# Moving the compressed projections, splitting a gate, and preparing branch weights one tile ahead in a one-core decoder trunk

## The chip, the cores and the metric

The kernel runs on one core of one Trainium2 chip. The metric is the device time of one execution in microseconds (us). TensorE (PE) multiplies, VectorE (DVE), ScalarE (ACT) and GpSimd (POOL) do the elementwise work, and SyncE (SP) issues most of the transfers from and to device memory. Everything is float32; nearly every matrix product is made of three products of rounded halves (a high part `hi` and the remainder `lo`), so each weight matrix has to be split by two instructions before it can be used: a cast on ACT that makes `hi`, and a subtraction that makes `lo`.

## The reference

One layer over 1024 tokens of width 1024: RMS norm, one input projection, three attention branches, a gated merge, an output projection, then a gated convolutional feed-forward. What the change touches is this:

```
kc = compress_blocks(k_cmp): blocks of 32 tokens, stride 16, + position; gelu(flat @ w1) @ w2
vc = compress_blocks(v_cmp): the same with its own weights
g = sigmoid(gates)                       # 3 x 1024 channels
merged = g0 * (y_a @ w_pa) + g1 * (y_b @ w_pb) + g2 * (y_c @ w_pc)
x = x + merged @ w_o
```

`y_a`, `y_b` and `y_c` are 256, 384 and 384 wide.

## The kernel before

Features lie on the partitions and tokens along the free axis, in two halves of 512. The program has stages in this order: an opening (norm, transposes), the input projections in pairs, the compressed projections with their two MLPs, attention, the branch outputs (`branch`, L1751), the last two gates, the merge (`merge`, L1766), the output projection, the feed-forward.

Inside the attention stage, and in a few others, the order of each engine's instructions is written out by a planner in the kernel (`Flow`), and TensorE's order there is fixed by it. In the compressed stage, and from the branch outputs to the first half of the output projection, the framework orders each engine's instructions instead: it takes them by their place in the program, but lets a later one go first when it expects an earlier one not to be ready. All orders are fixed when the kernel is built; on the chip each engine and each queue runs its own list in order.

`dense` (L784) takes the next 128 columns of the input projection's weights, which `next_w` has split one step ahead, and makes two halves of 24 products of 512 columns each, into the two PSUM banks with the tag `dn`. `dense_fm` (L302), which the merge uses, takes its banks from a rotation over all eight instead (`bank_tile`, L291).

**The compressed stage** (L2208 to L2212) is: `compress_in(0)` (project k, then split it into eight operands), `compress(0)` (its MLP), `compress_in(1)` (project v), `gate(2)`, `compress(1)`. `compress` (L1502) loads the 2 MB of first-layer weights in four parts. A part goes into a tile `raw` (tag `q1`, two buffers), is cast into `k1` and its remainder put into `k2` (two buffers each), and then feeds 12 products of 256 columns. After the fourth part come GELU, two transposes, a copy, two small products and a few copies. The tags `q1`, `q2`, `k1`, `k2`, `v`, `pc` and `p0` to `p5` are those of the attention stage: its first loads of queries, keys and values wait until the compressed stage has given these buffers up. Attention's own TensorE list begins with gate 3 (`fill`, products at L1700) and then the first scores.

**The merge** runs over eight tiles of 128 output columns. For each tile and each branch, `wprep` (L266) loads the branch's weights (SP), casts them (ACT, L274) and subtracts (POOL, L276), with two buffers each for `wr`, `wh` and `wl`. The gate's 128 x 1024 values are loaded into `gr` (three buffers; SP, L1773) and go through a sigmoid (ACT, L1774). The branch's products follow, 12 or 18 of 512 columns, and for each half of the tokens one or two instructions on DVE (L1780, L1782, L1783). The third branch ends with a cast and a subtraction that write the merged operand (L1785, L1786). In tiles 2 to 5 `wo_part` (L1790) also loads, casts and subtracts (POOL, L1796) a quarter of the first half of `w_o`; the second half follows after the merge.

Of the kernel before, what the change touches and what calls it, by code (L numbers as in the profile page):

```python
# [6 lines left out]
F32 = mybir.dt.float32  # L7
F32R = mybir.dt.float32r
BF16 = mybir.dt.bfloat16
AF = mybir.ActivationFunctionType  # L10
ALU = mybir.AluOpType
# [4 lines left out]
P = 128  # L16
# [217 lines left out]
class Trunk:  # L234
# [548 lines left out]

    def dense(self, evac):  # L784
        w = self.next_w()
        for hh in range(2):
            ps = self.psA.tile([P, 512], F32, "dn")
            for k in range(8):
                self.mm3(ps, (w[0][:, k], w[1][:, k]), (self.hT[hh][0][:, k], self.hT[hh][1][:, k]), k == 0, k == 7)
            evac(hh, ps)  # L790
# [675 lines left out]
    def compress_in(self, which):  # L1466

        nc = self.nc
# [23 lines left out]
        for x in range(2):  # L1492
            for y in range(2):
                fv = fs[x].rearrange("p a g c -> p (a g c)")[:, y * 512:y * 512 + 512]
                f = self.ap.tile([P, 2, 512], F32R, f"p{2 * x + y}")
                fh, fl = f[:, 0], f[:, 1]
                nc.scalar.copy(fh, fv)
                nc.vector.tensor_tensor(fl, fv, fh.bitcast(F32), ALU.subtract)
                out.append((fh, fl))
        return out  # L1500

    def compress(self, which, fq):  # L1502

        nc, ap = self.nc, self.ap
# [5 lines left out]
        for p4 in range(4):  # L1510
            raw = ap.tile([P, 4, 256], F32, "q1")
            hi = ap.tile([P, 4, 256], F32R, "k1")
# [150 lines left out]

    def gate(self, f):

# [10 lines left out]

        self.dense(evac)

# [87 lines left out]
    def merge(self, pool, ys, f, out):  # L1766

        nc, a = self.nc, self.a
        acc = pool.tile([P, S], F32, "acc")
        for br, (w, kk) in enumerate(((a["w_pa"][0], 2), (a["w_pb"][0], 3), (a["w_pc"][0], 3))):  # L1770
            wt = self.wprep([w[:, f * P:(f + 1) * P]], kk, P)
            gt = pool.tile([P, S], F32, "gr")
# [14 lines left out]

            self.dense_fm(wt, lambda k, hh: (yh[:, k, hh * 512:hh * 512 + 512], yl[:, k, hh * 512:hh * 512 + 512]), kk, evac)

    def wo_part(self, wo, nh, k):  # L1790
# [4 lines left out]
        nc.scalar.copy(wo[0][:, k:k + 2], raw)  # L1795
        nc.gpsimd.tensor_tensor(wo[1][:, k:k + 2], raw, wo[0][:, k:k + 2].bitcast(F32), ALU.subtract)  # L1796

# [388 lines left out]
    def run(self):  # L2186
# [20 lines left out]
        self.wspec = wl  # L2207
        fq = self.compress_in(0)  # L2208
        self.compress(0, fq)
        fq = self.compress_in(1)  # L2210
        self.gate(2)
        self.compress(1, fq)  # L2212
        self.psum_pool(True)
# [119 lines left out]
```

## Time and profile before

| | us |
|---|---|
| median of 3 runs (lowest, highest) | 1694.63 (1693.8, 1695.72) |
| the profiled execution | 1694.78 |
| its span (first to last instruction) | 1693.0 |
| busy: TensorE, VectorE, ScalarE, GpSimd | 1644.5, 1306.0, 835.7, 419.1 |

The profile lists instructions with start and duration, and gives the idle time ahead of one on its engine with what ended it. A product's end is modelled; the spacing of starts tells more. Products of 512 columns that follow one another at full clock start 0.23 us apart while each is shown 0.39 us long, so a gap of 0.6 us between two starts is a loss of some 0.4 us, of which the trace calls only 0.2 idle.

### The profile page before, as it was taken

To read this page: it belongs to the slowest core of one execution; us is meant where nothing else is said; L and a number is where in the kernel's file an instruction comes from. 1 tells how busy PE (TensorE), PEld (TensorE's weight loads), DVE (VectorE), ACT (ScalarE), POOL (GpSimd) and SP (SyncE) were. 2 spreads that over 40 slices of the span, in tenths; PEclk is the share of its full clock that TensorE was granted. 3 is DMA by queue.
4 is the path that set the end of the run, shared out by engine and by line. 5 is a ranking of instruction groups with operands and counts; after the bars stand their busy time and mean duration, and the time that the engine had idled before them with its cause. 6 is when DMAs were issued, how large, how long until landed. Compare 5 with 4: busy or idle time off the path is not lost.

```text
span 1693.0 us, 24484 instructions
## 1 busy us (share of the span) xinstructions
PE 1644.5 (97%) x8456; PEld 1367.5 (81%) x8456; DVE 1306.0 (77%) x2292; ACT 835.7 (49%) x1612; POOL 419.1 (25%) x323
## 2 busy tenths in 40 slices
PE   6989999998999999999999999999999999999998
PEld 6878888877888888888876788888888888888886
DVE  8976676553888889889477427999999999865774
ACT  6433443223878877788544314433333333454461
POOL 2232322321000011110034300165555645100020
PEclk9999999999999999999999999999999999999999
DMA  6545665367467664671466600255445544487671
GB/s 206 157 121 153 171 172 164 106 157 187 111 163 186 161 165 116 167 206 52 143 218 207 246 28 13 75 184 171 169 146 186 183 157 147 159 262 229 207 256 51
DMA packets 226058, 269.10 MB, mean 159 GB/s; under 512 B 21184, under 2 KB 162070, under 8 KB 225726
## 3 DMA queue, kind: packets, MB, share of 16 engines
q1 hardware_dynamic: 223262, 259.52, 51.5%
q0 software_dynamic: 1088, 4.88, 0.9%
q10 hardware_dynamic: 1584, 3.15, 0.5%
q8 instruction: 67, 1.10, 0.3%
q14 instruction: 57, 0.47, 0.1%
HBM read 188.26 MB, written 81.93 MB: 160 GB/s over the span
## 4 chain that ended last, share of the span: by engine, by line
PE 62%; DVE 21%; issue 6%; DMA 5%; ACT 3%; POOL 1%; SPq 0%; DVEq 0%; POOLq 0%; ACTq 0%
PE X L1700 6%; PE dn L298 5%; PE dn L299 5%; PE dn L300 5%; PE S L300 4%; PE S L299 4%; PE S L298 4%; PE X L1150 4%; DVE t L1975 3%; PE T L300 3%; PE T L298 3%; PE T L299 3%; DVE u L2036 2%; PE PV L1197 2%; PE S L1052 2%
## 5 line engine op out<-in xcount | busy, mean ns | idle before, releaser
L1169 DVE TENSOR_TENSOR tl<-X,th 128x512 fp32r<-128x512 f32 (+2 forms) x202 | 116.5, 586 | 14.9 <-ACT th L1166 12.7
L1166 ACT CAST th<-X 128x512 fp32r<-128x512 f32 (+2 forms) x202 | 101.3, 508 | 34.8 <-PE X L1150 31.9
L1736 POOL TENSOR_TENSOR wl<-wr,wh 128x256 fp32r<-128x256 f32 x44 | 33.5, 794 | 307.4 <-ACT wh L1731 292.6
L1076 DVE TENSOR_REDUCE sm<-S 128x1 f32<-128x640 f32 (+7 forms) x128 | 87.6, 712 | 22.0 <-PE S L1052 21.1
L1975 DVE SCALAR_TENSOR_TENSOR t<-u,ccols,t 128x511 f32<-128x511 f32 (+1 forms) x88 | 94.4, 1072 | 6.6 <-ACT t L1970 5.5
L1150 PE MATMUL X<-ident,p 128*128 128x128 f32 x610 | 97.7, 275 | 0.5 <-DVE tl L1169 0.3
L1084 ACT ACTIVATE p<-S,sm 128x640 f32<-128x640 f32 (+7 forms) x128 | 90.7, 713 | 13.6 <-DVE sm L1076 12.9
L1196 PE MATMUL PV<-th,v 128*128 128x256 f32 (+1 forms) x362 | 94.3, 283 | 0.1
L1052 PE MATMUL S<-k,q 98*128 98x128 f32 (+6 forms) x240 | 89.6, 382 | 1.0 <-issue 1.0
L1197 PE MATMUL PV<-tl,v 128*128 128x256 f32 (+1 forms) x362 | 89.5, 281 | 0.6 <-DVE tl L1169 0.5
L1048 PE MATMUL S<-k,q 128*128 128x512 f32 (+2 forms) x240 | 81.5, 340 | 2.2 <-ACT p L1084 2.1
L1150 PEld LDWEIGHTS X<-ident,p 128*128 128x128 f32 x610 | 70.3, 140 | 8.3 <-DVE tl L1169 1.0
L1700 PE MATMUL X<-hTh,wh 128*128 128x512 f32 x176 | 73.7, 419 | 2.2 <-DVE vcs L1551 2.1
L1900 POOL TENSOR_TENSOR su<-wr 128x512 f32<-128x512 f32 x20 | 32.1, 1606 | 168.6 <-DMA wr<-w_up 76.4
L276 POOL TENSOR_TENSOR wl<-wr,wh 128x384 fp32r<-128x384 f32 (+2 forms) x29 | 39.6, 1369 | 136.0 <-ACT wh L274 113.3
L1700 PE MATMUL X<-hTh,wl 128*128 128x512 f32 x176 | 73.1, 415 | 0.0
L1700 PE MATMUL X<-hTl,wh 128*128 128x512 f32 x176 | 72.9, 414 | 0.0
L1197 PEld LDWEIGHTS PV<-tl,v 128*128 128x128 f32 x362 | 68.5, 189 | 4.9 <-DVE tl L1169 1.9
L1196 PEld LDWEIGHTS PV<-th,v 128*128 128x128 f32 x362 | 68.5, 189 | 4.0 <-DVE y L1217 2.2
L1976 ACT ACTIVATE t<-t 128x512 f32<-128x512 f32 x44 | 27.8, 633 | 83.9 <-DVE t L1975 83.9
L298 PE MATMUL dn<-hTh,wh 128*128 128x512 f32 x152 | 59.7, 393 | 2.8 <-ACT f L1672 2.1
L300 PE MATMUL S<-blk,wh 128*128 128x512 f32 x152 | 60.1, 395 | 0.2 <-DVE wh L1912 0.2
(817 smaller groups left out, 5533.6 us busy)
## 6 DMA issues: line engine op xcount, KB each, us to landing
wr<-w_up SPq DMA_DIRECT2D x66, 256.0 KB
gr<-dg SPq DMA_DIRECT2D x24, 512.0 KB
t<-w_down SPq DMA_DIRECT2D x22, 512.0 KB
dt<-t SPq DMA_DIRECT2D x22, 512.0 KB
wr<-w_in SPq DMA_DIRECT2D x40, 256.0 KB
wr<-dl SPq DMA_DIRECT2D x39, 256.0 KB
wr<-w_in SPq DMA_DIRECT2D x18, 512.0 KB
x<-x SPq DMA_DIRECT2D x16, 512.0 KB
```

Source lines behind the costliest of these rows:

```text
L298: nc.tensor.matmul(out, st[0], mv[0], start=first, stop=False)
L299: nc.tensor.matmul(out, st[0], mv[1], start=False, stop=False)
L300: nc.tensor.matmul(out, st[1], mv[0], start=False, stop=last)
L1052: nc.tensor.matmul(out, q.t[1][0:R, qs], k.t[1][0:R, cs], start=False, stop=True)
L1084: nc.scalar.activation(o.rearrange("p a b -> p (a b)"), u, AF.Exp, bias=mx[:, x:x + 1], accum_out=sm[:, 2 + x:3 + x])
L1150: nc.tensor.transpose(ps[:, n * P:(n + 1) * P], b(), self.ident)
L1166: nc.scalar.copy(g.th[:, cs], ps[:, cs])
L1169: yield "DVE", 0, 0.07 + cs.stop * 1.04e-3, lambda: nc.vector.tensor_tensor(g.tl[:, cs], ps[:, cs], g.th[:, cs].bitcast(F32), ALU.subtract)
L1196: nc.tensor.matmul(unit.pv[:, oc], w, g.th[:, cs], start=first and i == 0, stop=False)
L1197: nc.tensor.matmul(unit.pv[:, oc], w, g.tl[:, cs], start=False, stop=e)
L1700: nc.tensor.matmul(p, w[i][:, k], self.hT[hh][j][:, k], start=x == 0, stop=x == 23)
L1975: nc.vector.scalar_tensor_tensor(o, i, cw[2 - sh], o, ALU.mult, ALU.add)
```

## The change

`compress_in` runs for k and for v before either MLP; the operands of v get buffers of their own (tags `q2` and `v`). The second half of gate 2 comes after the MLP of v in the program, the first half ahead of it. The MLP's raw weights take four buffers (`q1` and `pc`, two each) in place of two. `dense` takes its banks from the rotation. In the merge, the three branches' weights of a tile are one operand, loaded by three transfers, cast by one instruction and subtracted by one on DVE; it is made after the first branch's products of the tile before. `wo_part` subtracts on DVE.

```diff
-    def dense(self, evac):
+    def dense(self, evac, between=None):
         w = self.next_w()
         for hh in range(2):
-            ps = self.psA.tile([P, 512], F32, "dn")
+            if hh and between:
+                between()
+            ps = self.bank_tile()
...
-                f = self.ap.tile([P, 2, 512], F32R, f"p{2 * x + y}")
+                f = self.ap.tile([P, 2, 512], F32R, (f"p{2 * x + y}", ("q2", "v")[x])[which])
...
-            raw = ap.tile([P, 4, 256], F32, "q1")
+            raw = ap.tile([P, 4, 256], F32, ("q1", "pc")[p4 // 2])
...
-        for br, (w, kk) in enumerate(((a["w_pa"][0], 2), (a["w_pb"][0], 3), (a["w_pc"][0], 3))):
-            wt = self.wprep([w[:, f * P:(f + 1) * P]], kk, P)
+        if f == 0:
+            self.merge_weights(0)
+        hi, lo = self.mw
+        for br, (k0, kk) in enumerate(((0, 2), (2, 3), (5, 3))):
+            wt = hi[:, k0:k0 + kk], lo[:, k0:k0 + kk]
...
+            if br == 0 and f < 7:
+                self.merge_weights(f + 1)
+
+    def merge_weights(self, f):
...
+        raw = self.wp.tile([P, 8, P], F32, "wr")
+        for n, k0, k1 in (("w_pa", 0, 2), ("w_pb", 2, 5), ("w_pc", 5, 8)):
+            nc.sync.dma_start(raw[:, k0:k1], a[n][0][:, f * P:(f + 1) * P].rearrange("(k p) n -> p k n", p=P))
+        self.mw = hi, lo = self.wp.tile([P, 8, P], F32R, "wh"), self.wp.tile([P, 8, P], F32R, "wl")
+        nc.scalar.copy(hi, raw)
+        nc.vector.tensor_tensor(lo, raw, hi.bitcast(F32), ALU.subtract)
...
-        nc.gpsimd.tensor_tensor(wo[1][:, k:k + 2], raw, wo[0][:, k:k + 2].bitcast(F32), ALU.subtract)
+        nc.vector.tensor_tensor(wo[1][:, k:k + 2], raw, wo[0][:, k:k + 2].bitcast(F32), ALU.subtract)
...
-        fq = self.compress_in(0)
-        self.compress(0, fq)
-        fq = self.compress_in(1)
-        self.gate(2)
-        self.compress(1, fq)
+
+        fq = [self.compress_in(x) for x in range(2)]
+        self.compress(0, fq[0])
+        self.gate(2, lambda: self.compress(1, fq[1]))
```

## Rows read from the trace of the kernel before

**Rows 1.** The page's first part: busy time, share of the span and instructions of each engine.

```profile
PE 1644.5 (97%) x8456; PEld 1367.5 (81%) x8456; DVE 1306.0 (77%) x2292; ACT 835.7 (49%) x1612; POOL 419.1 (25%) x323
```

**Rows 2.** Windows of 20 us: length, busy time and instructions of PE, PEld, DVE, ACT, POOL, then TensorE's granted clock (1.00 is 2.4 GHz), busy share of the transfer engines, GB/s.

```profile
360.00:380.00 20.00, 18.53 (x97) 15.32 (x97) 15.05 (x31) 7.33 (x9) 2.67 (x3) 1.00 0.84 192
400.00:420.00 20.00, 15.85 (x73) 12.97 (x74) 3.96 (x7) 2.73 (x7) 2.52 (x2) 0.91 0.89 209
...
840.00:860.00 20.00, 16.25 (x70) 12.46 (x69) 11.10 (x12) 11.45 (x15) 3.23 (x4) 1.00 0.88 288
...
920.00:940.00 20.00, 17.75 (x73) 13.01 (x72) 15.35 (x21) 8.54 (x13) 8.30 (x6) 1.00 0.58 190
980.00:1000.00 20.00, 20.00 (x89) 16.44 (x89) 2.22 (x4) 0.00 (x0) 0.00 (x0) 1.00 0.00 1
```

**Rows 3.** TensorE in order of time through the compressed stage: start, duration, engine, line, operation, output and inputs; in brackets the idle time ahead and what ended it. The first is the first product of the stage, L1700 is gate 3 in the attention stage; the last two have 32 products between them.

```profile
355.07 0.39 PE L298 MATMUL dn<-hTh,wh 128*128 128x512 f32 x1
...
371.65 0.39 PE L298 MATMUL S<-k,p 128*128 128x256 f32 x1 [1.47 <-ACT p L1497]
...
401.03 0.39 PE L299 MATMUL S<-k,p 128*128 128x256 f32 x1 [1.20 <-DVE k L1517]
...
403.87 0.28 PE L299 MATMUL S<-k,p 128*128 128x256 f32 x1
403.99 0.28 PE L300 MATMUL S<-k,p 128*128 128x256 f32 x1
404.75 0.44 PE L1528 MATMUL T<-ident,y 128*128 128x128 f32 x2 [0.47 <-ACT y L1524]
405.70 0.66 PE L1542 MATMUL T<-cw,y 128*128 128x64 f32 x4 [0.52 <-DVE y L1529]
408.49 0.47 PE L1700 MATMUL X<-hTh,wh 128*128 128x512 f32 x1 [2.13 <-DVE vcs L1551]
...
409.95 0.63 PE L1700 MATMUL X<-hTh,wh 128*128 128x512 f32 x1
...
413.36 0.39 PE L1700 MATMUL X<-hTh,wl 128*128 128x512 f32 x1
...
420.84 0.39 PE L1700 MATMUL X<-hTh,wl 128*128 128x512 f32 x1
```

**Rows 4.** A window of 1 us in that stretch, columns as in rows 2.

```profile
410.00:411.00 1.00, 1.00 (x4) 0.81 (x3) 0.00 (x0) 0.00 (x0) 0.00 (x0) 0.50 1.07 297
```

**Rows 5.** The elementwise work of the compressed stage: the two lines that split a part of the first-layer weights (duration in ns, least, median, most), and from DVE's timeline the four subtractions that split k and the eight additions that evacuate half a projection.

```profile
L1516 ACT CAST k<-q x8: 1045/1047/1054, 365.8 to 399.8; 128x1024 fp32r<-128x1024 f32 x8
L1517 DVE TENSOR_TENSOR k<-q,k x8: 1224/1226/1748, 366.9 to 400.9; 128x1024 fp32r<-128x1024 f32 x8
372.41 2.49 DVE L1498 TENSOR_TENSOR p<-p,p 128x512 fp32r<-128x512 f32 x4
377.02 3.04 DVE L1486 TENSOR_TENSOR p<-dn,pb 64x256 f32<-64x256 f32 x8
```

**Rows 6.** SP's timeline, the first loads of attention's values and keys, and TensorE's first score.

```profile
392.13 0.44 SPq L1018 DMA_DIRECT2D v<-dv_a  x1
402.65 0.46 SPq L1009 DMA_DIRECT2D k<-dk_a  x1
421.07 0.22 PE L1048 MATMUL S<-k,q 128*128 128x128 f32 x1
```

**Rows 7.** TensorE in order of time from the last gate to the output projection: the wait inside the last gates, the first product of the merge, the wait for `y_c`, the first product after the merge.

```profile
841.91 0.39 PE L300 MATMUL dn<-hTh,wl 128*128 128x512 f32 x1
844.43 0.50 PE L298 MATMUL dn<-hTh,wh 128*128 128x512 f32 x1 [2.13 <-ACT f L1672]
...
850.00 0.39 PE L298 MATMUL PV<-yh,wh 128*128 128x512 f32 x1
...
865.13 0.50 PE L298 MATMUL S<-yh,wh 128*128 128x512 f32 x1 [1.40 <-ACT yh L1762]
...
950.53 0.39 PE L298 MATMUL dn<-blk,blk 128*128 128x512 f32 x1
```

**Rows 8.** Waits from 849 to 951 us: who waited for whom, us in total, times, the longest.

```profile
PE S L300 <- POOL wl L276: 2.6, 5, 0.7
PE PV L300 <- POOL wl L276: 1.8, 3, 1.0
PE S L298 <- ACT yh L1762: 1.4, 1, 1.4
PE S L298 <- ACT wh L274: 1.2, 1, 1.2
```

**Rows 9.** Elementwise lines of the merge (ns, least, median, most), and one instruction of DVE's timeline with the idle time ahead of it.

```profile
L1796 POOL TENSOR_TENSOR blk<-wr,blk x8: 2397/2414/2456, 884.8 to 968.2; 128x1024 fp32r<-128x1024 f32 x8
L1783 DVE TENSOR_TENSOR acc<-acc,gr x32: 682/693/2893, 857.9 to 952.0; 128x512 f32<-128x512 f32 x32
907.37 0.69 DVE L1786 TENSOR_TENSOR blk<-acc,blk 128x512 fp32r<-128x512 f32 x1 [3.92 <-ACT blk L1785]
```

**Rows 10.** Pieces of the chain of waits in the merge (start, us, what): one gate load, its sigmoid, and the next load that the same chain leads to.

```profile
892.41 5.62 DMA gr<-dg
898.05 1.07 ACT gr L1774
...
901.90 3.85 DMA gr<-dg
```

More of the change, by code (lines that the diff above doesn't have):

```diff
@@ L1661, in nsa_rows, with gate @@
         self.poke()
-    def gate(self, f):
+    def gate(self, f, between=None):
         nc = self.nc
@@ L1675, in evac @@
             nc.scalar.dma_start(self.dg[f][:, cs], gt)
-        self.dense(evac)
+        self.dense(evac, between)
     def fill(self):
@@ L1788, in merge @@
             self.dense_fm(wt, lambda k, hh: (yh[:, k, hh * 512:hh * 512 + 512], yl[:, k, hh * 512:hh * 512 + 512]), kk, evac)
+            if br == 0 and f < 7:
+                self.merge_weights(f + 1)
+    def merge_weights(self, f):
+        nc, a = self.nc, self.a
+        raw = self.wp.tile([P, 8, P], F32, "wr")
[4 more added lines that the diff above has]
+        nc.vector.tensor_tensor(lo, raw, hi.bitcast(F32), ALU.subtract)
     def wo_part(self, wo, nh, k):
```

## The prediction

> **What bounds the kernel now.** The page's first part, read first, says that TensorE is busy for 97% of the span [rows 1]; no other engine passes 77%. So the time is TensorE's work plus its gaps, and the question is where the gaps are. The windows of 20 us, read next, put them in two places that the change touches: from 360 to 420 us (1.5 and 4.2 us idle in two of the windows) and from 840 to 940 us (3.8 and 2.3 us), while in a settled window TensorE is busy for all of 20 us [rows 2]. Busy time hides part of the loss, since a product is shown longer than the spacing at which they follow. I therefore count starts: 33 steps in 420.84 - 413.36 = 7.48 us, 0.2267 us for each product of 512 columns, and 0.12 us for one of 256 [rows 3].
>
> *Compressed stage.* From the first projection product at 355.07 to gate 3 at 408.49 are 53.42 us [rows 3]. The work in it is 144 products of 512 columns (k, v and gate 2, 48 each), 32.6 us; 96 of 256 columns in the two MLPs, 11.5; and two tails of transposes and small products, 0.44 + 0.66 each, 2.2. Together 46.3, so 7.1 us are lost: 1.5 while TensorE waits for the split of k, 1.2 for a remainder of the weights, and most of the rest in the bare tail of the second MLP, whose last large product starts at 403.99 while gate 3 starts only at 408.49. The gap has an aftermath: the granted clock at 410 is 0.50, the lower of its two levels [rows 4], and gate 3's eight products from 409.95 to 413.36 take 3.41 us in place of 8 x 0.2267 = 1.81 [rows 3]. That is 1.6 us more.
>
> *Gates and merge.* Inside the last gates TensorE waits for a `dn` bank: 844.43 - 841.91 - 0.23 = 2.3 us [rows 7]. The merge has 8 x 48 = 384 products, 87.0 us, and takes 950.53 - 850.00 = 100.5 [rows 7]; 13.5 are lost. One gap of 1.4, with its slow restart 1.7, is the wait for `y_c`; the waits that the trace names are otherwise for weights, remainder first and cast second [rows 8]. I put the other 11.8 us down to weights that are ready just in time or late.
>
> **The change part by part.**
>
> *Order of the compressed stage.* No product is added or removed. k's and v's 96 products now run back to back, 21.8 us, to about 376.8. The split of k, which TensorE waited for, is over at 372.4 + 2.5 = 374.9 [rows 5] and goes under v's products, so those 1.5 us go. What is late next is the split of v: its buffers `p4` and `p5` are those of k, so its additions (3.0 us for each half [rows 5]) begin after 374.9, and with the split it is ready near 384 to 386. The first MLP (6.8 us with its tail) and gate 2's first half (24 x 0.2267 = 5.4) lie on TensorE in that time. Each MLP is also held to its splits: two buffers of `k1` and `k2`, one part a cast of 1.05 us and a subtraction of 1.22 [rows 5] against 12 x 0.12 = 1.4 us of products. So the third and fourth parts wait up to 2.3 us each, and a gate half is there to fill these waits. Of the second half's 5.4 us I expect 1.6 to be used so and 3.8 to be left for the tail of 408.49 - 403.99 = 4.5 us. With 0.7 for the rest of the tail and 0.5 for small waits, gate 3 starts at 355.1 + 46.3 + 1.2 = 402.6, 5.9 us earlier, and without the lower clock another 1.6 is saved: 7.5. Bounds: 8.7 if nothing is left bare; 2.5 if the gate's half is spent before the tail and the clock falls as before (7.1 - 4.5).
>
> *The extra raw buffers* let four parts be requested at once. They take nothing from TensorE; they make the 2 MB land earlier, while the transfer engines are at 0.84 [rows 2]. I count nothing, from -0.5 to +0.5 us.
>
> *Loads moved behind.* v's operands now sit in the buffers into which attention's first `q2` and `v` go, so the load of values issued at 392.13 [rows 6] moves behind the second MLP's products; the first keys (402.65 [rows 6]) were behind them already. On SP everything after them in the list waits too. Before, the keys are issued 18 us ahead of the first score at 421.07 [rows 6]. After, the MLP ends near 396 and the first score is due near 402.6 + 10.9 + 0.5, again 18 us later. About 1.5 MB more has to land in that time and 1 MB less (`q1` is free earlier); at 209 GB/s [rows 2] 0.5 MB is 2.4 us. Cost 0, at worst 2.4.
>
> *The bank rotation in `dense`* removes the 2.3 us in the last gates. The evacuation is as late as before, but the next half goes into another bank. It also shifts the rotation for all that follows; -1 to +1, taken as 0.
>
> *Branch weights.* Per tile, three casts, three subtractions on POOL and their waits become one cast of 1024 columns on ACT (1.05 us for that shape [rows 5]) and one subtraction on DVE (1.22 [rows 5]), made a tile of 10.9 us ahead. The two buffers of `wh` and `wl` allow it: tile f+1 takes those of tile f-1, free when tile f begins. So all 11.8 us can go. The subtractions of `w_o` leave POOL, where each takes 2.4 us and holds up additions of DVE (L1783: median 0.69, most 2.89 [rows 9]), for 1.22 us of DVE. DVE's sum for a tile is then 4 pairs of multiply and add, 4 x 1.35, two multiplies and two subtractions at 0.6, and the new one, in tiles 2 to 5 two: 5.4 + 2.4 + 1.2 to 2.4 = 9.0 to 10.2 us, under the 10.9 of the products. The pair's 1.35 and the 0.6 are my estimates, from L1783's median of 0.69 less the overlap of successive instructions.
>
> *What is late next in the merge.* First `y_c`, at 865.1 [rows 7] and set by transfers (288 GB/s before 860 [rows 2]). TensorE reaches it earlier, but with a whole tile of weights ahead it has the second tile's first two branches, 30 products or 6.8 us, to do meanwhile; I add 0.5 us, at worst 4.6 (the 2.3 of the gates and the 2.2 of weight waits before it). Second the gate loads: three buffers, one per branch, so each goes round once per tile. One round in the trace is 901.90 - 892.41 = 9.5 us [rows 10], with a transfer of 5.6, longer than the next one's 3.9. That is under 10.9, but the same bytes have to come in fewer us. I take a mean of 11.25 per tile in place of 10.88, 3.0 us over eight tiles; from 0 to 9 (12.0 per tile).
>
> *Sum.* Compressed stage 7.5; gates 2.3; merge 11.8 - 0.5 - 3.0 = 8.3. Together 18.1 us from the profiled execution's 1694.78, 1.8 of which lies outside the span and stays: 1676.7, and since that execution is 0.15 above the median, 1676.5. Everything after either stage is work of TensorE that moves forward as it is, since its loads are released by buffers that come free earlier too.
>
> **The rivals.**
>
> *The gate loads take the weights' place.* For: a round of 9.5 us, and DVE's and ACT's instructions of several tiles in one line each. Against: the weights' own waits were ahead of the loads in SP's line, and they go. At 12.0 us per tile and 4.6 us at `y_c`, the merge comes to 11.8 - 4.6 - 9.0 = 1.8 us worse than now, and the time is 1694.6 - 7.5 - 2.3 + 1.8 = 1686.6.
>
> *The compressed stage gives nothing back.* The framework's order decides how gate 2's halves are spread; in the order before, too, gate 2 was there to fill the second MLP, and its tail was bare. Then 2.5 or less is saved there, and 10.6 in gates and merge: 1681.5.
>
> *The change doesn't do what it says.* If the next tile's cast and subtraction are placed late in ACT's and DVE's lists, weights are just in time as now; with a bare tail as well, 1690 to 1695.
>
> *Slower: DVE's line becomes the bound of the merge.* It runs in order, and a subtraction that waits for its cast holds all behind it: 3.92 us idle ahead of the one at 907.37 [rows 9]. With such a wait in each tile beside the larger sum of 10.2 us of work, a tile takes 14.1 us, 25.8 over eight tiles above the products; against the 13.5 lost now that costs 12.3, the rest saves 9.8, and the time is 1697. It decides from 100.5 + 9.8 over 8 = 13.8 us per tile. Against it: these waits are DVE's spare time while TensorE is late, and eight banks let TensorE run some 14 us ahead.
> The Trainium skill states the general case ("TensorE: Matmul & The Clock Gate", section "Architectural detail: the array is 16× 32×32, not 1× 128×128"): the queues of ScalarE and VectorE are strictly first in, first out. The 3.92 us agree with that; by this rule alone, work moved from the idle POOL to DVE can only wait longer.
>
> **How the numbers follow.** The forecast has 0.53 (own range 1671 to 1682); gate loads 0.19; compressed stage 0.13; not as it says 0.09; DVE 0.06. The two partial rivals still are faster. A measurement tells about 0.2%, 3.4 us, from no change, so faster means below 1691.2: 0.53 + 0.19 + 0.13 and a little of the next, 0.86; the same 0.08; slower 0.06. The range runs from 1670, all bounds at their best (8.7 + 2.3 + 11.8 gives 1671.8, less 1 for the banks), to 1688, past the first two rivals.
>
> **What would show it.** Gate 3 starts at 401 to 404, with clock 1.00 in its first products; no wait of TensorE for the split of k. No gap of over 1 us between the two last gates. In the merge no wait for a subtraction of weights, POOL without work, DVE 80 to 95% busy, and 88 to 92 us for the 384 products but for the wait at `y_c`. I am wrong if TensorE waits there for banks (the gate loads or DVE), if a bare tail of over 2 us stands ahead of gate 3, or if the first scores start over 13 us after gate 3.

## The result, and the profile after

The changed kernel takes 1682.4 us (median of 3 runs, 1680.1 to 1683.23) against 1694.63: a ratio of 0.9924, 95% interval 0.9902 to 0.9947. Run once more beside other kernels it took 1681.6 (ratio 0.9922, 0.9908 to 0.9936). The forecast was 1676.5 with a range of 1670 to 1688: the right direction, and a third of the forecast gain missing. The profiled execution took 1682.4, 12.4 us under that of before.

The page's first part, after; it answers to [rows 1]:

```profile
PE 1640.5 (98%) x8456; PEld 1371.0 (82%) x8456; DVE 1308.5 (78%) x2308; ACT 832.0 (50%) x1596; POOL 371.9 (22%) x291
```

The same 8456 products; POOL loses 47 us, DVE gains 2.5. The place of the 12.4 us is read from starts. TensorE in order of time through the compressed stage, after (L1702 is gate 3, L1050 the first score; compare [rows 3, 6]):

```profile
355.00 0.39 PE L298 MATMUL PV<-hTh,wh 128*128 128x512 f32 x1
...
376.76 0.28 PE L298 MATMUL S<-k,p 128*128 128x256 f32 x1
...
402.06 0.39 PE L300 MATMUL dn<-hTh,wl 128*128 128x512 f32 x1
402.29 0.39 PE L1702 MATMUL X<-hTh,wh 128*128 128x512 f32 x1
...
413.17 0.22 PE L1050 MATMUL S<-k,q 128*128 128x128 f32 x1
```

The first MLP's product at 376.76 waits for nothing, gate 3 follows gate 2's last product at the usual 0.23 us, and its 48 products and the score come at full rate. And from the last gates to the output projection (compare [rows 7]):

```profile
820.06 0.39 PE L298 MATMUL T<-hTh,wh 128*128 128x512 f32 x1
...
841.60 0.39 PE L300 MATMUL dn<-hTh,wl 128*128 128x512 f32 x1
841.82 0.39 PE L298 MATMUL S<-yh,wh 128*128 128x512 f32 x1
...
849.58 0.39 PE L300 MATMUL T<-yh,wl 128*128 128x512 f32 x1
853.02 0.50 PE L298 MATMUL T<-yh,wh 128*128 128x512 f32 x1 [3.05 <-ACT yh L1764]
854.28 0.80 PE L299 MATMUL T<-yl,wh 128*128 128x512 f32 x1 [0.76 <-DVE yl L1765]
...
857.63 0.39 PE L298 MATMUL PV<-yh,wh 128*128 128x512 f32 x1
...
860.36 0.39 PE L298 MATMUL S<-yh,wh 128*128 128x512 f32 x1
861.67 0.50 PE L298 MATMUL T<-yh,wh 128*128 128x512 f32 x1 [0.93 <-ACT yh L1764]
...
936.39 0.39 PE L298 MATMUL dn<-blk,blk 128*128 128x512 f32 x1
```

No gap is left inside the last gates or between them and the merge. The merge takes 936.39 - 841.82 = 94.6 us for 87.0 of products, and nearly the whole difference stands at `y_c`: 3.2 + 1.0 + 1.1 us of gaps, and in between eight products in 857.63 - 854.28 = 3.35 us in place of 1.81. A window of 1 us shows the clock there: behind the gap it is granted at 0.50, the lower level (columns as in [rows 2]).

```profile
855.00:856.00 1.00, 1.00 (x4) 0.82 (x3) 0.96 (x2) 0.00 (x0) 0.00 (x0) 0.50 1.15 295
...
862.00:936.00 74.00, 74.00 (x328) 61.26 (x327) 65.04 (x96) 38.02 (x44) 0.00 (x0) 1.00 0.68 218
```

The last row is the merge behind `y_c`: TensorE without a gap, DVE at 65.04 of 74 us, POOL without work. The whole list of TensorE's waits from 841 to 937 us has three lines, while [rows 8] are only the first of a longer one:

```profile
PE T L298 <- ACT yh L1764: 4.0, 2, 3.1
PE T L299 <- DVE yl L1765: 0.8, 1, 0.8
PE S L300 <- DVE wl L1805: 0.2, 1, 0.2
```

The table holds the same stretches for all runs, from TensorE's starts in each profiled execution (us): A from the first projection product to the first score, B from there to the last gates, C the last gates and the merge, D from the first product of `w_o` to the last product. The time is the median of the kernel's runs in that comparison; ratios are to the kernel before on the same chip. The kernel before itself took 1693.47 to 1696.2 us in the later comparisons, so ratios can be compared across the table better than times.

| kernel | time | ratio, 95% interval | A | B | C | D |
|---|---|---|---|---|---|---|
| before | 1694.63 | | 66.0 | 404.8 | 124.7 | 734.5 |
| changed | 1682.4 | 0.9924 (0.9902, 0.9947) | 58.2 | 406.9 | 116.3 | 736.3 |
| changed, again | 1681.6 | 0.9922 (0.9908, 0.9936) | 58.2 | 408.3 | 116.9 | 736.7 |
| 1 compressed stage only | 1689.3 | 0.9965 (0.9952, 0.9978) | 58.1 | 406.8 | 124.3 | 734.5 |
| 2 weights only | 1688.17 | 0.9960 (0.9947, 0.9973) | 66.9 | 405.8 | 115.2 | 736.3 |
| 3 last gates on two banks | 1680.42 | 0.9917 (0.9904, 0.9930) | 58.3 | 404.5 | 116.9 | 736.0 |
| 4 two tiles | 1682.11 | 0.9936 (0.9917, 0.9955) | 58.4 | 403.3 | 116.1 | 736.3 |
| 5 four summand buffers | 1677.11 | 0.9906 (0.9888, 0.9924) | 58.2 | 404.4 | 111.8 | 736.1 |
| 6 both 4 and 5 | 1681.51 | 0.9926 (0.9908, 0.9943) | 58.1 | 406.5 | 116.4 | 736.8 |
| 7 `lo` on GpSimd | 1684.38 | 0.9949 (0.9930, 0.9968) | 58.3 | 408.7 | 121.0 | 736.9 |
| 8 gate 2 whole | 1683.96 | 0.9928 (0.9907, 0.9948) | 60.8 | 404.2 | 116.8 | 735.6 |
| 9 two gate buffers | 1688.27 | 0.9943 (0.9921, 0.9965) | 58.2 | 407.2 | 116.8 | 741.1 |
| 10 both 3 and 5 | 1679.92 | 0.9902 (0.9886, 0.9917) | 58.1 | 406.7 | 112.3 | 735.3 |
| 11 five summand buffers | 1675.39 | 0.9880 (0.9860, 0.9900) | 58.3 | 406.7 | 108.8 | 737.4 |

A and C answer to the edits and vary by less than 1 us otherwise: A is 58.1 to 58.4 in the eleven executions with the whole new stage, and 66.0 and 66.9 in the two with the old one. B varies by 5 us between executions whatever the edit (last section), so one profiled time alone says little about 3 us.

### The profile page after: what moved, and what is told of

The parts are those of the page before. It is cut to its first block, busy times and chain, and to the rows that moved or that the text cites. A ratio compares the mean times of both kernels' runs of the same rounds, so it can differ in the third digit from the quotient of the medians.

```text
span 1680.6 us, 24436 instructions
## 1 busy us (share of the span) xinstructions
PE 1640.5 (98%) x8456; PEld 1371.0 (82%) x8456; DVE 1308.5 (78%) x2308; ACT 832.0 (50%) x1596; POOL 371.9 (22%) x291
## 4 chain that ended last, share of the span: by engine, by line
PE 70%; DVE 16%; DMA 4%; issue 4%; ACT 2%; POOL 2%; SPq 0%; DVEq 0%; POOLq 0%; ACTq 0%
PE X L1702 6%; PE S L299 6%; PE S L300 6%; PE S L298 6%; PE dn L298 5%; PE dn L299 5%; PE dn L300 5%; PE X L1152 4%; PE T L300 4%; PE T L298 4%; PE T L299 4%; PE PV L1199 2%; PE S L1054 2%; PE PV L1198 2%; DVE t L1992 2%
## 5 line engine op out<-in xcount | busy, mean ns | idle before, releaser
L1171 DVE TENSOR_TENSOR tl<-X,th 128x512 fp32r<-128x512 f32 (+2 forms) x202 | 116.4, 585 | 16.0 <-ACT th L1168 13.9
L1050 PE MATMUL S<-k,q 128*128 128x512 f32 (+2 forms) x240 | 81.9, 341 | 2.1 <-ACT p L1086 1.5
L1702 PE MATMUL X<-hTh,wh 128*128 128x512 f32 x176 | 72.8, 414 | 0.0
L1702 PE MATMUL X<-hTh,wl 128*128 128x512 f32 x176 | 72.6, 413 | 0.0
L1702 PE MATMUL X<-hTl,wh 128*128 128x512 f32 x176 | 72.3, 411 | 0.0
L1928 ACT CAST wh<-wr 128x512 fp32r<-128x512 f32 x53 | 32.6, 616 | 60.3 <-POOL wr L1921 39.5
L300 PE MATMUL S<-blk,wh 128*128 128x512 f32 x156 | 61.0, 391 | 1.5 <-DVE wh L1929 1.5
L299 PE MATMUL S<-blk,wh 128*128 128x512 f32 x156 | 61.4, 394 | 0.0
```

The lines of the kernel that those rows point to most:

```text
L299: nc.tensor.matmul(out, st[0], mv[1], start=False, stop=False)
L300: nc.tensor.matmul(out, st[1], mv[0], start=False, stop=last)
L1171: yield "DVE", 0, 0.07 + cs.stop * 1.04e-3, lambda: nc.vector.tensor_tensor(g.tl[:, cs], ps[:, cs], g.th[:, cs].bitcast(F32), ALU.subtract)
L1702: nc.tensor.matmul(p, w[i][:, k], self.hT[hh][j][:, k], start=x == 0, stop=x == 23)
```

## The experiments

**The changed kernel again**, as a reference for what follows.

> The changed kernel once more. Two losses in its first trace are in none of the terms of the prediction: an idle stretch of 1.9 us in TensorE's line at 540 us of the attention stage with the lower clock behind it, 2.3 us in all, and two waits of 1.1 and 1.2 us for subtractions on VectorE in the feed-forward, 1.8 us more than before. Theory 1, both come and go from run to run: here the shift against the kernel before stays 7.9 us through attention, or the waits in the feed-forward are elsewhere, and single runs differ by 2 to 3 us. Theory 2, both are lasting costs of the new order and placement: the same two places, the same sizes within 0.5 us, and a median of 1682 to 1683 us. Either way 6 to 7 us are lost at the wait for y_c between 849 and 862 us.

Measured: 1681.6 us, and all three losses are there again: idle 3.33, 0.77 and 0.87 us at `y_c`, a gap of 1.72 us at 541.93 with the lower clock behind it, waits of 1.2 and 1.1 us for the line L1929 in the feed-forward. The places are those of Theory 2. But the loss at 540 us is not of the same size (B is 408.3 against 406.9), and runs 3, 4 and 5, whose edits lie behind attention, don't have the fall of the clock at all (last section): that loss comes and goes. The waits in the feed-forward stay.

**1 and 2. The parts alone.** Run 1 keeps the new order of the compressed stage and takes back the rest (`merge` and `wo_part` of before, last gates on `dn`); run 2 is the kernel before with the new `merge`, `merge_weights` and `wo_part`.

> The changed order of the compressed stage alone (both projections ahead of the MLPs, gate 2 split, four raw buffers, bank rotation there); the last two gates and the merge as in the kernel before. If the terms add up: the first score 7.9 us earlier and a time of 1686.7 us, or 1689 us if the loss at 540 us belongs to the order. If instead the gain of this stage is given back later in attention, because loads of queries, keys and values come later, the last gates start less than 5 us earlier and the time is above 1690 us.

> The merge's weights as one operand a tile ahead and all subtractions of the merge and of w_o on VectorE, and nothing else of the change (last gates on two banks). Theory 1, the weights' 11.8 us go and the wait for y_c takes back what TensorE arrives early by: it arrives 2.3 us later than in the changed kernel, so the wait with its slow clock costs 4 to 5 us in place of 1.7, and the time is 1685 to 1687 us. Theory 2, VectorE or the gate loads bound the merge in part and the changed kernel's trace shows that only beside the other edits: more than 2 us lost after 870 us, and above 1688 us.

Run 1 saves 66.0 - 58.1 = 7.9 us in A and 0.4 in C; its 1689.3 us is the second figure of its expectation, and its trace has the loss at 540 us. Run 2 saves 124.7 - 115.2 = 9.5 in C and nothing in A (66.9). So the parts hardly touch each other. In run 2 the merge itself takes 88.4 us, 1.3 over its products: nearly all of the 11.8 us of weight waits are gone, but its last gates take 26.8 instead of 24.2. Where TensorE waits 3.3 us in the gates it waits only 1.0 us for `y_c`. Neither theory of run 2 foresaw this: its 1688.17 us is above the range of Theory 1, which put the wait at `y_c`, and nothing is lost in the merge after 871 us, which Theory 2 asked for.

**3. The bank rotation.** Changed kernel, last gates on the two `dn` banks:

```diff
-            ps = self.bank_tile()
+            ps = self.psA.tile([P, 512], F32, "dn") if self.late else self.bank_tile()
```

> The changed kernel with the last two gates on the two banks dn again. The prediction gave the bank rotation there 2.3 us. If that step stands, this kernel is 2.3 us slower than the changed one, 1684.7 us. Rival: y_c is ready at a time set by transfers, so what TensorE wins in the gates it waits longer for y_c; then the wait in the gates comes back with 2 us, the wait for y_c shrinks by about as much (and the clock may not fall), and the time is that of the changed kernel within 0.7 us.

The rival: C is 116.9, as with the rotation (116.3 and 116.9). TensorE waits 4.4 us for a bank, more than the 2 expected, and then only 1.5 for `y_c`. Its list of waits, last gates and merge:

```profile
PE dn L299 <- ACT f L1675: 4.4, 1, 4.4
PE S L299 <- ACT yh L1765: 1.5, 1, 1.5
```

So in the changed kernel the rotation is worth nothing: what it saves is waited again at `y_c`, a little further on. ACT's list in this run shows that both waits have one root:

```profile
836.70 1.04 ACT L1765 CAST yh<-gr 128x1024 fp32r<-128x1024 f32 x1 [1.71 <-DMA gr<-dy_b]
837.65 0.68 ACT L1675 ACTIVATE f<-dn,cols 128x512 f32<-128x512 f32 x1
```

The instruction that empties the bank (L1675) stands in ACT's list behind casts of branch operands that wait for their loads.

**4 to 6. What sets `y_c`.** Either TensorE had nothing else in line when it got there, or the operands come late. Run 4 puts the second tile's first two branches ahead of the first tile's third one; run 5 gives the loads of the branch operands a fourth buffer; run 6 does both.

```diff
-        for f in range(8):
-            self.merge(gp, ys, f, mt)
+        for f in range(2):
+            self.merge(gp, ys, f, mt, (0, 1))
+        self.merge(gp, ys, 0, mt, (2,))
+        self.merge_weights(2)
+        self.merge(gp, ys, 1, mt, (2,))
+        for f in range(2, 8):
+            self.merge(gp, ys, f, mt)
```

```diff
-        self.st = Pool(self, "last", {"gr": 3, "f0": 2, "f1": 2}, side="right")
+        self.st = Pool(self, "last", {"gr": 4, "f0": 2, "f1": 2}, side="right")
```

> The changed kernel with one reordering: the first two branches of the second output tile are issued ahead of the third branch of the first tile (and the weights of the third tile after that), so that 80 products which need only branches 1 and 2 stand in front of the wait for branch 3. Theory A (what stands in line at the wait for branch 3 sets its price: in the changed kernel TensorE meets the wait with nothing left to do and 5 to 6 us go, idle and at half clock): the last gates and the merge together go from 116.3 to 110.5 to 113 us and the time to 1677 to 1680. Rival B (the arrival of branch 3 sets the end of the merge, whatever stands in front of it): 116 to 117 us and 1681 to 1683. Rival C (more tiles in flight hold the three gate buffers, and the loads behind them wait): over 117.5 us, 1683 or more.

> The changed kernel with four buffers instead of three for the summands of the branches ahead of the last gates, so that the last loads of branch 3 don't wait for a buffer whose sum, cast and subtraction are still to be done. Theory A (the loads of branch 3 queue on these buffers): its last operand is there 2 to 4 us earlier, the loss at the wait for branch 3 falls from 5 to 6 us to 1 to 3, time 1678 to 1680. Rival B (the transfers' own length sets the arrival): no change, 1681 to 1683.

> Both of the last two edits together. If each takes away a part of the same wait, the wait is gone: last gates and merge together 109.5 to 111.5 us, time 1675.5 to 1678, not lower than the better of the two by more than 2 us. If the wait isn't set by either, 1681 to 1683.

Run 4 gains nothing: C 116.1, rival B. Its TensorE goes on working to 853.97, then waits for the last operand of `y_c`:

```profile
856.61 0.51 PE L298 MATMUL S<-yh,wh 128*128 128x512 f32 x1 [2.48 <-ACT yh L1764]
```

That is 41.5 us behind the start of its last gates (815.09); in the changed kernel the last operand's first product starts at 861.67, 41.6 us behind 820.06. The arrival has not moved, and it bounds the end. That C comes out the same is in part chance: run 4 has 66 products of the merge ahead of that point, the changed kernel 55, which is 2.5 us less to do behind it, and run 4 loses nearly as much again behind the gap, 1.0 us on a wait for the operand's remainder and 1.4 at the lower clock.

Run 5 moves the arrival. The three additions that make `y_c` (count, ns least, median, most, then first and last start), changed kernel (last gates from 820.06):

```profile
L1763 DVE TENSOR_TENSOR gr<-gr,gr x3: 1217/1226/1229, 845.3 to 858.3; 128x1024 f32<-128x1024 f32 x3
```

and with four buffers (last gates from 817.43):

```profile
L1763 DVE TENSOR_TENSOR gr<-gr,gr x3: 1225/1225/1226, 838.5 to 846.7; 128x1024 f32<-128x1024 f32 x3
```

The last one begins 38.3 us behind the start of the gates in the one and 29.3 in the other; C falls by 4.5 to 111.8. This is Theory A. SP's list of the changed kernel shows the mechanism:

```profile
841.05 0.32 SPq L1760 DMA_DIRECT2D gr<-dy_c  x1
842.58 0.38 SPq L1802 DMA_DIRECT2D wr<-w_pa  x1
...
846.59 0.34 SPq L1762 DMA_DIRECT2D gr<-dy_c  x1
848.93 0.34 SPq L1760 DMA_DIRECT2D gr<-dy_c  x1
...
852.32 0.42 SPq L1762 DMA_DIRECT2D gr<-dy_c  x1
```

A load of `y_c` is issued when a buffer is free, that is when an earlier operand is summed, or summed, cast and subtracted. The load at 846.59 goes out as the first addition of `y_c` ends, which began at 845.34 and takes 1.23 us, the load at 852.32 shortly after the end of the second, which began at 850.67. The weights of the second tile, and between 848.93 and 852.32 those of the third, stand ahead of the last loads in the fixed list; by these times the third tile's cost the last load some 0.4 us, and the rest is the wait for buffers. With four buffers the last load is issued at 842.08, 24.7 us behind the start of the gates in place of 32.3, and ahead of the second tile's weights.

In run 6 the gain is gone (C 116.4), although the last operand of `y_c` is cast early here too, at 852.69, 31.4 us behind the start of the gates. TensorE's waits in its gates and merge:

```profile
PE T L300 <- DVE wl L1808: 3.7, 1, 3.7
PE T L298 <- ACT wh L1807: 1.8, 1, 1.8
```

It now asks for the second tile's weights early, and these wait behind `y_c` twice: their loads go out from 846.70 on, after the last load of `y_c` at 845.38, and their subtraction starts only at 855.03, 3.2 us after their cast has ended, behind an addition and a subtraction of `y_c` and two multiplications in VectorE's list. The expectation's last clause has the size, but not the reason: both edits act on the wait at `y_c`, and another wait takes its place.

**7. The engine of the subtractions.** Back on GpSimd, still one operand a tile ahead:

```diff
-        nc.vector.tensor_tensor(lo, raw, hi.bitcast(F32), ALU.subtract)
+        nc.gpsimd.tensor_tensor(lo, raw, hi.bitcast(F32), ALU.subtract)
...
-        nc.vector.tensor_tensor(wo[1][:, k:k + 2], raw, wo[0][:, k:k + 2].bitcast(F32), ALU.subtract)
+        nc.gpsimd.tensor_tensor(wo[1][:, k:k + 2], raw, wo[0][:, k:k + 2].bitcast(F32), ALU.subtract)
```

> The changed kernel with the lo halves of the branch weights and of w_o on GpSimd, as before, but still as one operand a tile ahead. My theory of the merge: the tile's lead hides the subtraction on either engine, so the merge stays within 1 us of the changed kernel's, full rate after the wait for branch 3. Rival: GpSimd's subtraction of a whole operand is late by what the four of before were late, merge 4 to 8 us longer, 1686 to 1690. For the stretch from the first product of w_o to the end, which is 1.5 to 2.2 us longer in every kernel that has the weights' part of the change: if the place of these subtractions is the cause it goes back from 736.3 to 734.5 us (time about 1680 where the merge stays); if not it stays at 736 to 737.

C is 121.0, 4 to 5 us longer: the rival, at the low end (its time of 1684.38 us is below the rival's range). TensorE's waits for GpSimd's subtraction in the merge are 3.1 and 0.6 us in total. The longest, 1.7 us, is for the first tile's own weights, which have no lead. The last one, from POOL's list and TensorE's:

```profile
930.47 2.52 POOL L1805 TENSOR_TENSOR wl<-wr,wh 128x1024 fp32r<-128x1024 f32 x1 [10.06 <-ACT wh L1804]
```

```profile
933.04 0.50 PE L300 MATMUL S<-yh,wl 128*128 128x512 f32 x1 [1.41 <-POOL wl L1805]
```

POOL was idle and began as soon as the cast was there, so the operand wasn't a tile ahead in this tile: its cast stands late in ACT's list, and then 2.5 us instead of DVE's 1.2 count in full. DVE's additions show a second price. First this run, then the changed kernel, where POOL does nothing in the merge:

```profile
L1788 DVE TENSOR_TENSOR acc<-acc,gr x32: 678/692/2890, 856.5 to 949.7; 128x512 f32<-128x512 f32 x32
```

```profile
L1788 DVE TENSOR_TENSOR acc<-acc,gr x32: 682/688/693, 854.1 to 937.8; 128x512 f32<-128x512 f32 x32
```

The longest takes 2890 ns beside a working GpSimd (L1805 takes 2358 to 2844) and 693 without. The additions of 2.9 us in this run each lie beside one of these subtractions and end some 0.55 us after it. The Trainium skill ("Trainium Architecture — The Big Picture", section "What this means for kernel authors") says that VectorE and GpSimd share a pair of ports and that the one that holds it shuts the other out instead of sharing the rate; the two rows agree. D stays long at 736.9, so these subtractions don't cause its 1.8 us.

**8. The gate round the second MLP.**

```diff
-        self.gate(2, lambda: self.compress(1, fq[1]))
+        self.gate(2)
+        self.compress(1, fq[1])
```

> The changed kernel with gate 2 in one piece ahead of the second compressed MLP (both projections still ahead of both MLPs). My theory of the compressed stage: the split of k stays hidden, but the second MLP's tail is bare again, some 3.8 to 4.5 us, and the clock falls behind it (1.6 us more), so gate 3 starts 3.5 to 4.5 us later after the first projection product than in the changed kernel and the first score 5 to 6 us later; time 1686 to 1688. Rival: moving both projections ahead is what pays, and the split of the gate round the second MLP adds nothing: first score within 1 us of the changed kernel's, 1681 to 1683.

A is 60.8, 2.6 us longer: neither. TensorE at the second MLP's end:

```profile
400.12 0.39 PE L299 MATMUL S<-k,v 128*128 128x256 f32 x1 [1.21 <-DVE k L1519]
...
402.86 0.28 PE L300 MATMUL S<-k,v 128*128 128x256 f32 x1
403.61 0.44 PE L1530 MATMUL T<-ident,y 128*128 128x128 f32 x2 [0.47 <-ACT y L1526]
404.56 0.66 PE L1544 MATMUL T<-cw,y 128*128 128x64 f32 x4 [0.52 <-DVE y L1531]
405.03 0.48 PE L1702 MATMUL X<-hTh,wh 128*128 128x512 f32 x1
```

The tail is bare but 2.2 us long instead of 4.5: gate 3 follows its last product directly, where before it waited another 2.13 us for a copy [rows 3], and the clock stays up (1.00 in every window of 1 us from 404 to 411). So of the 7.8 us 2.6 come from splitting the gate and 5.2 from the rest of the change in this stage: both projections ahead of both MLPs, four raw buffers, `dense` on the rotation. By the rows these 5.2 are the wait for the split of k (1.5), the wait for the copy (2.1) and the aftermath at the lower clock (1.6). Only the first is shown to come from the order. Which of the three parts removes the wait for the copy was not tried and stays open. In the time (ratio 0.9928) the 2.6 us drown in the variation of B.

**9. The round of the gate loads.** Two buffers `gr` in place of three in the merge:

```diff
-        gp = Pool(self, "gp", {"gr": 3, "acc": 2})
+        gp = Pool(self, "gp", {"gr": 2, "acc": 2})
```

> The changed kernel with two buffers instead of three for the gates that the merge loads. My prediction priced these loads by a round of 9.5 us per buffer, three buffers for three loads per tile; if that round is needed work, two buffers make a tile 14.2 us, the merge 25 us longer, time 1705 to 1710. Rival: most of the round is a loaded gate waiting for its products, so a shorter round is possible: at 7.3 us per round two buffers still hold 10.9 us per tile, merge 0 to 5 us longer, 1682 to 1687.

Nearer the rival, but not as it says: 1688.27 us, no loss in C, 4.8 us more in D. ACT's list shows the pace in this run (every third sigmoid, three per tile):

```profile
895.19 1.06 ACT L1779 ACTIVATE gr<-gr 128x1024 f32<-128x1024 f32 x1 [3.77 <-DMA gr<-dg]
...
907.06 1.06 ACT L1779 ACTIVATE gr<-gr 128x1024 f32<-128x1024 f32 x1 [3.79 <-DMA gr<-dg]
...
919.16 1.06 ACT L1779 ACTIVATE gr<-gr 128x1024 f32<-128x1024 f32 x1 [3.72 <-DMA gr<-dg]
```

A tile takes 12.0 us here, so with two buffers for three loads a round needs 12.0 x 2 / 3 = 8.0 us, not 9.5; with three buffers 8.0 per tile would do, under the 10.9 of the products. The sigmoids fall behind the products by 1.1 us per tile, and DVE's work on the products with them; the eight banks let TensorE run ahead, and the debt shows at the output projection, where TensorE waits 1.0 us for `acc` ahead of the first product and 2.1 for `blk` behind it. Some 3 of the 4.8 us arise there; the rest are longer waits in the feed-forward, which vary in all kernels.

**10 and 11. The rotation once `y_c` is early, and a fifth buffer.** Run 10 is run 5 with run 3's edit. In run 11 the fifth buffer is paid for with the gates' output buffers:

```diff
-        self.st = Pool(self, "last", {"gr": 3, "f0": 2, "f1": 2}, side="right")
+        self.st = Pool(self, "last", {"gr": 5, "f0": 1, "f1": 1}, side="right")
```

> Four buffers for the summands of the branches, as in the run that made the changed kernel faster, but with the last gates on their two banks of before. Theory A (the bank rotation was worth nothing only because TensorE then waited longer for branch 3): with branch 3 there earlier, the 2 to 4.5 us that the gates wait for a bank are covered only by the 2.4 us that are left at branch 3, so last gates and merge together go from 111.8 to 113 to 115 us, time 1678 to 1681. Rival B (the rotation is worth nothing in any case): 111.5 to 112.5 us, 1676 to 1678.

> Five buffers for the summands of the branches, paid for with one buffer in place of two for each half of a gate's output. If buffers still hold back the loads of branch 3, its wait of 2.4 us goes: last gates and merge 109 to 110.5 us, time 1674 to 1676. If the transfers themselves are now the bound (the engines show 0.9 and more all through that stretch), the wait stays: 111 to 112.5 us, 1676 to 1678. If the single output buffers hold up the last gates, those take over 22.5 us and it is slower than with four.

Run 10: C 112.3, rival B by this stretch, but not for its reason. (Its time of 1679.92 us lies in Theory A's range because B has the fall of the clock here and not in run 5: 406.7 against 404.4.) The wait for a bank doesn't come back at all: the gates take 22.0 us on two banks, and TensorE's waits in gates and merge are

```profile
PE S L299 <- ACT yh L1765: 1.8, 1, 1.8
PE S L300 <- DVE yl L1766: 0.9, 1, 0.9
```

With loads that come in time ACT is free to empty the banks: the same two banks cost 4.4 us in run 3 and nothing here, and the summand buffer is the only difference. The missing buffer was behind that wait too.

Run 11, the first of its three outcomes: C 108.8, that is 21.8 for the gates and 87.04 for the merge, the bare time of 384 products (384 x 0.2267 = 87.05); from 815 to 952 us TensorE's list of waits is empty. SP's list:

```profile
839.65 0.32 SPq L1762 DMA_DIRECT2D gr<-dy_c  x1
840.02 1.65 SPq L1778 DMA_DIRECT2D gr<-dg  x3
```

The last load of `y_c` goes out 20.2 us behind the start of the gates (819.43), ahead of all gate loads, and the single output buffers don't hold up the gates. At 1675.39 us and a ratio of 0.988 (0.986 to 0.990) this kernel beats the one before and the changed one; its interval lies wholly below the changed kernel's second measurement (0.9908 to 0.9936).

## Why the prediction was right, and by how much it was wrong

The direction and the range held. The time alone would not have shown that: 1682.4 us is within 1 us of the rival with the bare compressed stage (1681.5), which A refutes and the time doesn't. (Two small sums of the working are 0.1 off: 7.1 - 4.5 is 2.6, and 2.3 + 2.2 is 4.5. Nothing hangs on them.) Term by term, on the profiled executions:

| term | forecast | measured |
|---|---|---|
| compressed stage (A) | 7.5 | 7.8 |
| last gates (24.2 to 21.8) | 2.3 | 2.4 |
| merge (100.5 to 94.6) | 8.3 | 6.0 |
| attention (B) | 0 | -2.1 |
| from `w_o` on (D) | 0 | -1.8 |
| sum, rounded | 18.1 | 12.3 |

- *Compressed stage*: right in size and mechanism. Gate 3 at 402.29 (forecast 402.6) at clock 1.00, no wait for the split of k, the first score 10.9 us behind it, and run 1 shows the saving by itself. The loads that move behind cost nothing up to the first score. Run 8 corrects one part: for the whole gate I expected a loss of 5 to 6 us, it was 2.6, because the wait for the copy was already gone.
- *Bank rotation*: right as a row (2.4 us less in the gates), wrong as a term. Runs 3 and 10 show it worth about half a microsecond at most in either setting. I had read the wait as a matter of banks; ACT's casts behind late loads were its cause, which run 10 shows by removing it with earlier loads on the same two banks.
- *Weights*: right. Run 2 brings the merge to 88.4 us, and no wait for a cast or subtraction of over 0.2 us is left in the changed kernel's.
- *Gate loads*: mis-sized. I took 3.0 us; measured 0, since TensorE has no gap from 862 to 936 us. Only with two buffers (run 9) does the round bind. The 9.5 us of [rows 10] were one round in a stretch in which the buffer also waited for its branch, not the least it needs: run 9 goes round in 8.0.
- *`y_c`*: this step failed. "with a whole tile of weights ahead it has the second tile's first two branches, 30 products or 6.8 us, to do meanwhile; I add 0.5 us, at worst 4.6". Before, the wait cost 1.7 us; after, 3.2 + 1.0 + 1.5 (lower clock) + 1.1 = 6.9, so 5.2 more. Three things were wrong. First, the order: in TensorE's fixed list the third branch's second operand stands ahead of the second tile, whose first product comes only at 857.63. The lower end of my working rested on an order that the trace of before doesn't show; but run 4 shows that the other order gains next to nothing, since the operand comes 41.5 us behind the start of the gates, whatever is done meanwhile. Second, I had called the arrival set by transfers; run 5 shows that it is set by when the loads are issued, and that by the summand buffers. Third, I had taken it as fixed, and it comes later after the change. So the worst end, all that was saved ahead of the wait, was the better number, and still too low. The last gates of before start here:

```profile
825.82 0.39 PE L298 MATMUL dn<-hTh,wh 128*128 128x512 f32 x1
```

The wait at 865.13 [rows 7] ends 39.3 us behind that, in the changed kernel 41.6 us behind the start of the gates: 2.3 later. (In run 1, with the old merge, it is 38.5; in run 2, with the new one, 40.4.) Of the 2.3 us 1.3 are the last addition, which begins 38.3 us behind the start in place of 37.0. The other 1.0 is the cast that follows it. In ACT's list it now stands behind a sigmoid:

```profile
859.63 1.06 ACT L1779 ACTIVATE gr<-gr 128x1024 f32<-128x1024 f32 x1 [6.66 <-DVE gr L1763]
860.59 1.03 ACT L1764 CAST yh<-gr 128x1024 fp32r<-128x1024 f32 x1
```

So from the start of the gates to this operand the changed kernel takes 2.3 us longer and has done five products (1.1 us) more by then. All the gain of C lies behind `y_c`.

The two errors in the merge partly cancel (3.0 - 4.7); with 0.6 of small gaps that leaves 2.3 of the missing 5.8 us there. Another 2.1 is B: a longer gap in attention and a fall of the clock behind it, which the profiled execution of before doesn't have and five of the others don't either (last section). The last 1.8 is D: 735.3 to 737.4 us in all kernels with the weights' part and three gate buffers, against 734.5 in both without. The order of the instructions of TensorE, VectorE, ScalarE and GpSimd there is the same before and after, but for the last subtractions of `w_o`, which change from GpSimd to VectorE; what differs is small waits of the feed-forward, as these two rows of the changed kernel's list of waits from 936 us on (the same line costs TensorE 0.6 us there before):

```profile
PE S L300 <- DVE wh L1929: 1.5, 2, 1.0
PE T L300 <- DVE wh L1929: 0.9, 1, 0.9
```

Run 7 excludes the engine of the subtractions. Why these waits come with this part of the change stays open.

Of the rivals, the one on gate loads had its second half right (4.6 us at `y_c`) and its first wrong; DVE's line, at 88% busy, did not become the bound, since no product of the changed kernel's merge waits more than 0.2 us for a subtraction of weights. The rule of the Trainium skill that spoke for it ("TensorE: Matmul & The Clock Gate", section "Architectural detail: the array is 16× 32×32, not 1× 128×128": the queues of ScalarE and VectorE are strictly first in, first out) is seen at work elsewhere, in ACT's list of run 3, where the emptying of a bank stands behind a cast that waits for its load.

## What to carry to other kernels

When a gain lies ahead of a wait on a transfer, ask first what issues that transfer: unless the issue moves too, count the gain as nought, and check whether the change puts other work ahead of it. A load that waits for one of a few rotating buffers comes late, and with it the cast that uses it and whatever stands behind that cast in its engine's list; here a wait for PSUM banks and a wait for an operand had that one root, and two more buffers took 7.5 us from C, about as much as the new compressed stage took from A. A round read from a trace is an upper bound on what the loop needs: taking a buffer away shows whether less will do.

## What the runs showed of the hardware that was not expected

- The 5 us by which B varies are one gap of TensorE and its clock behind it. Some 130 us into attention a product waits 0.8 to 2.2 us in thirteen of the fourteen traces for something that the profile puts down to "issue"; run 4, which lacks the gap, has the shortest B. In the changed kernel, TensorE's row and a window of 1 us behind it:

```profile
542.46 0.30 PE L1054 MATMUL S<-k,q 98*128 98x128 f32 x1 [1.93 <-issue]
```

```profile
544.00:545.00 1.00, 1.00 (x6) 0.97 (x6) 1.00 (x3) 0.89 (x4) 0.00 (x0) 0.50 0.77 218
```

In eight of the fourteen profiled executions (the changed kernel in both, and runs 1, 6, 7, 9, 10 and 11) the granted clock then falls to 0.50 for some 3.5 to 7 us; there B is 406.5 to 408.7. In the other six (before, and runs 2, 3, 4, 5 and 8) it stays at 1.00, and B is 403.3 to 405.8. The gap's length alone doesn't decide: run 2 has 2.04 us without a fall, run 6 1.46 with one. All eight have the new order of the compressed stage, but so have four of the six, and in eleven executions the four engines run the same instructions in the same order up to there: eight of them have the fall, three (runs 3, 4 and 5) don't. Whether the new order makes the fall more frequent stays open, as does what the product waits for.

- At `y_c` the clock is a part of the price as well: behind the 3.05 and 0.76 us of idle time in the changed kernel the aftermath costs another 1.5, behind the 1.57 and 0.87 us at the same place in run 5 the products come at their usual spacing, at a granted clock of 1.00.
